# State space outputs by channels in a hybrid decoder layer: X as the left operand, z turned instead of y, and the norm's factor in the addition to h

## The chip, the cores and the metric

The kernel runs on one core of one Trainium2 chip. Times are microseconds of that core on the device, from the first to the last instruction of one execution with what the runtime counts around it; the figure that is compared is the median of several runs. TensorE is called PE, VectorE DVE, ScalarE ACT, GpSimd POOL and SyncE, which issues most transfers, SP.

## The reference

One layer of a decoder over T = 256 tokens of width 2048. All values are float32.

```
a    = RMSNorm(h)
[z | x,B,C | dt | q | k | v] = a @ W_in
x,B,C = SiLU(causal depthwise conv, 4 taps)
SSD  : per chunk of 128 tokens, group g (4), head (8 per group, 64 channels each):
         X      = x * dt
         a_cs   = cumsum(dt * A)                      along the chunk
         y_diag = (C B^T * exp(a_cs[l] - a_cs[s]) for s <= l) @ X
         state  = B^T @ (X * exp(a_cs[last] - a_cs))  of the chunk before
         y_off  = exp(a_cs) * (C @ state)             second chunk only
       y = y_diag + y_off + d_skip * x ;  y = y * SiLU(z)
       y = y * rsqrt(mean(y^2 over the group's 512 channels) + eps) * gain
Attn : per-head RMSNorm of q and k, rotary, window of 128, sinks
h    = h + concat(y, attention) @ W_out
h    = h + (SiLU(g) * u) @ W_down,  [g | u] = causal conv(RMSNorm(h) @ W_up)
h    = h + sigmoid(RMSNorm(h) @ W_pg) * RMSNorm(p @ W_pe)
```

## The kernel before

Every product with a weight matrix is made of three TensorE products of a number format that is faster than float32: each operand is split into a high and a low part, and hi*hi, hi*lo and lo*hi are added. So each weight tile of 128 x 1024 (`w`) is loaded, its high part `wh` is made on ACT and its low part `wl` on DVE, and PE takes 12 products of 512 columns from it. There are seven raw weight buffers and four split ones. The left operands (`ah`/`al` for the layer's normed input, `yh`/`yl` for the inputs to W_out) hold channels on partitions, tokens along the row; a product has 128 tokens on PSUM partitions and 512 columns.

The kernel has four stages: a load phase (some 55 us), in which the input and the first weights arrive and B and C are projected; the state space stage; attention with the rest of the output projection; and the two feed-forward parts. In the load phase the loop over `k` (16 steps, line 835) issues on SP, at step 8, four small loads after each other: `wd`, `scw`, `rows` and `posi` (lines 853 to 856); at steps 5 and 9 it loads the two halves of h, and ACT squares each as it lands (line 862).

The state space stage is not issued in the order in which it is written. `Recorder` notes every operation with its operands (all of these instructions carry line 341 in the profile), `cost` gives each an assumed duration, and `solve` lists them per engine by due times; then they are issued in that fixed order. `ORDER` names the steps in the order in which they are recorded: `x0` (chunk of x of group 0, its convolution, decays and outputs), `z0` (its gate), `e0` (gate, norm and split of the result), `o0` (its part of the output projection), `r0` (rotary tables), `k0` (projection of the keys). Groups 1 to 3 go to W_out during attention.

In `ssd_x` a chunk comes out of PE with tokens on partitions. The convolution wants channels on partitions, so `turned` splits the 32-bit words into 16-bit halves on ACT (`half`), turns them with a transposing transfer (`SY.dma_start_transpose`), and joins them on ACT. After convolution and SiLU, `xc` is turned back in the same way. From it come `yc` = x * d_skip and `Xd` = x * dt, tokens on partitions. The products of a chunk are:

```
PE.matmul(yp[:, hs], lhsT=segs[c][:, h, :], rhs=Xd[c][:, hs], start=True, stop=True)   # 8 heads
PE.matmul(off, lhsT=CT[:, g, c * P : (c + 1) * P], rhs=prev, start=True, stop=True)    # second chunk
```

`segs` are the decays times C B^T, 128 x 128 a head; `prev` is the state of the first chunk. These are float32 products, two TensorE instructions each. `y` thus has tokens on partitions. `ssd_end` multiplies it by the gate, squares it on ACT with a sum along the row, scales it by the factor, turns it with two transposing transfers, and splits it with the gain as a per-partition scale. `TURNED` says what of x (`x`), of `xc` on the way back (`b`) and of y (`y`) is turned by transfers; `KEYS_DMA` says the same of B and C. B is turned by eight PE transposes, C by transfers.

Of the kernel before, what the change touches and what calls it, by code (L numbers as in the profile page):

```python
# [12 lines left out]
F32 = mybir.dt.float32  # L13
# [41 lines left out]
ROUNDS = 6  # L55
GBUF = 3
TAPS = (0,)
TURNED = ("xby", "xby", "xby", "xby")
KEYS_DMA = (False, True)
ORDER = "x0 r0 x1 z0 e0 x2 z1 e1 x3 o0 z2 e2 z3 e3 k0".split()  # L60
GATE_SECOND = [0, 1, 2, 3, 4, 5, 6, 7]


# [432 lines left out]
def cost(engine, method, args, kw, outs, ins):  # L496
    n = size(outs[0])
    if engine == "PE":
        if method == "transpose":
            return 0.11, 0.0  # L500
        if kw["lhsT"].dtype == F32R:
            return 0.0128 + 0.00042 * n, 0.0
        return 2 * max(0.105, 0.013 + 0.00042 * n), 0.0
    if engine == "SP":
        if method == "dma_start_transpose":
            return 1.0, 6.5
        return max(0.5, 2.0 * n / 1024), 2.2
# [18 lines left out]
def hybrid_layer(  # L526
# [122 lines left out]

    scw = sb(mc, [P, 24 * 5], "scw")  # L650
    rw = sb(mc, [P, 256], "rows")
    dtb, alog, dsk, sink = (rw[:, i * 32 : (i + 1) * 32] for i in range(4))
    qg, kg_ = rw[:, 128:192], rw[:, 192:256]
    g_attn, g_ffn, g_ple, g_ssm = (gn[:, i * KT : (i + 1) * KT] for i in range(4))
# [1 line left out]
    fcw = sb(const, [P, 88 * 4], "fcw")  # L656
    fill(mc)

    def rstd(ss, n, cols, tag):
        t = sb(small, [P, cols], "rs_t")  # L660
        V.tensor_scalar(t, ss, 1.0 / n, EPS, op0=ALU.mult, op1=ALU.add)
        r = sb(small, [P, cols], tag)
        G.tensor_tensor(out=r, in0=t, in1=nhalf[:, :cols], op=ALU.pow)
        return r

# [138 lines left out]
    def v3(a, m):  # L804
        return a.rearrange("p (a b) -> p a b", a=m)
# [7 lines left out]
    with xin_:  # L813
# [21 lines left out]
        for k in range(KT):  # L835
# [16 lines left out]
            if k == 8:  # L852
                nc.sync.dma_start(wd, w_dt)
                nc.sync.dma_start(scw, ssm_cw)
                nc.sync.dma_start(rw, rows.partition_broadcast(P))
                nc.sync.dma_start(posi, pos)
                split(wd, dhl[:, :, :32], dhl[:, :, 32:])
            if k in (5, 9):
# [26 lines left out]
            res.append(t)  # L885
        return res

    def add_to_h(acc, n):
        for b in range(NB):
            hs = hres[b][:, n * NC : (n + 1) * NC]  # L890
            V.tensor_tensor(out=hs, in0=hs, in1=acc[b], op=ALU.add)

    def squares(ss, n):

# [10 lines left out]
        V.tensor_reduce(out=s1, in_=ss, axis=AX.X, op=ALU.add)  # L905
        return rstd(s1, D, NB, tag)

    def project(lhs, w, i0, ni, after=None):

        for n in range(4):  # L910
            acc = acc_pair()
            gemm(acc, lhs, [w[i, n] for i in range(i0 * KG // KW, (i0 + ni) * KG // KW)])
            add_to_h(acc, n)
            if after:
                after(n)


    held = {}
# [3 lines left out]
    with tc.tile_pool(name="ssd", bufs=1) as sp, tc.tile_pool(name="dram", bufs=1, space=bass.MemoryType.DRAM) as dp:  # L922
# [32 lines left out]
        def turned(ts, tags):  # L955
            u = sb(sp, [P, 4, T], "uc")
# [53 lines left out]
        scr = plan.tile(dp, [64, P], "scr", lambda: dp.tile([64, P], F32, tag="scr", name="scr"), 1)  # L1010
        SY.dma_start(scr, acsT)
        eacs = sb(sp, [P, 64], "eacs")
        S.activation(out=eacs, in_=acs, func=AF.Exp)

        def ssd_x(g):
            segs = []
# [37 lines left out]
            y, Xd = [], []  # L1054
            for b in range(NB):
                yc = sb(sp, [P, NC], f"yc{b}", bufs=2)
# [18 lines left out]
            S.copy(prev, st)  # L1075
            for c in range(NB):
                yc = y[c]
                yp = ms_tile()
                with pe_group():
                    for h in range(8):  # L1080
                        hs = slice(h * HD, (h + 1) * HD)
                        PE.matmul(yp[:, hs], lhsT=segs[c][:, h, :], rhs=Xd[c][:, hs], start=True, stop=True)
                V.tensor_tensor(out=yc, in0=yc, in1=yp, op=ALU.add)
                if c:
                    off = ms_tile()
                    PE.matmul(off, lhsT=CT[:, g, c * P : (c + 1) * P], rhs=prev, start=True, stop=True)
                    t = sb(sp, [P, NC], "xe")
                    o = g * 16 + 8
                    V.tensor_tensor(out=v3(t, 8), in0=v3(off, 8), in1=bc(eacs[:, o : o + 8], HD), op=ALU.mult)
                    V.tensor_tensor(out=yc, in0=yc, in1=t, op=ALU.add)  # L1090
            return y

        def ssd_gate(g):
            acc = in_chunk(3 + 2 * g)
            zs = []
            for b in range(NB):
                z = sb(sp, [P, NC], f"z{b}")
                S.activation(out=z, in_=acc[b], func=AF.Silu, scale=rx[:, b : b + 1])
                zs.append(z)
            return zs  # L1100

        def ssd_end(g, y, zs):
            ssy = sb(sp, [P, NB], "ssy", bufs=2)
            for b in range(NB):
                V.tensor_tensor(out=y[b], in0=y[b], in1=zs[b], op=ALU.mult)
                S.activation(out=zs[b], in_=y[b], func=AF.Square, accum_out=ssy[:, b : b + 1])
            ry = rstd(ssy, NC, NB, "ry")
            for b in range(NB):
                V.tensor_scalar_mul(y[b], y[b], ry[:, b : b + 1])
            yT = Lhs(yp_, KG, "y")  # L1110
            gain = g_ssm[:, 4 * g : 4 * g + 4]
            if "y" in TURNED[g]:
                u = turned(y, ("z", "Xd"))
                for f in range(4):
                    h, l = yT.part(f)
                    split(u[:, f, :], h, l, gain[:, f : f + 1])
            else:
                transpose_split(y, yT, 0, gain)
            return (yT, w_out, g, 1)

        def rotary():
            rp = sp
# [53 lines left out]
            S.activation(out=cos_t, in_=kk, func=AF.Sin)  # L1176
            return sin_t, cos_t

        ys, zs = {}, {}
        for step in ORDER:  # L1180
            what, g = step[0], int(step[1])
# [26 lines left out]
    with tc.tile_pool(name="att_s", bufs=2) as as_, tc.tile_pool(name="att", bufs=2, reuse_waits="tile") as ap_, tc.tile_pool(name="ps_sc", bufs=1, space=PSUM) as ps_sc:  # L1208
        plan = Recorder(zip(("DVE", "ACT", "POOL", "PE", "SP"), real_engines), {AF.Exp}, before.rest, before)
        V, S, G, PE, SY = plan.V, plan.S, plan.G, plan.PE, plan.SY  # L1210
        keys_acc = [plan.carry(t, (ps_acc, f"acc{b}")) for b, t in enumerate(keys_acc)]
        for lhs, *_ in held.values():
            lhs.t = [tuple(plan.carry(t, (yp_, f"y{e}0"), F32R) for e, t in zip("hl", ts)) for ts in lhs.t]
        aT.t = [tuple(plan.keep(t, [P, KG, T], act, f"a{e}{g}", 1, dtype=F32R) for e, t in zip("hl", ts)) for g, ts in enumerate(aT.t)]
        hres = [plan.keep(t, [P, D]) for t in real_h]
        early = [tuple(plan.carry(t, (wp, f"w{e}"), F32R) for e, t in zip("hl", ts)) for ts in early]
# [132 lines left out]
        def values(j):  # L1349

            yT = Lhs(yp_, KG, "y")
            for b in range(NB):
# [17 lines left out]
            held[4 + j] = (yT, w_out, 4 + j, 1)  # L1370

        def chunk(c, then):
            acc = acc_pair()
# [5 lines left out]
                yield  # L1379

        def output(i):
            lhs, w, i0, ni = held.pop(i)
            for n in range(4):
                acc = acc_pair()
                for s in range(2):
                    products(acc, lhs, load_w(w[i0 * 2 + s, n]), s * KW, KW, KG, s == 1)
                    if s == 1:
                        add_to_h(acc, n)
                    yield

        at = {}
# [820 lines left out]
```

## Time and profile before

| what | us |
|---|---|
| median of 3 runs | 1386.87 (1386.06 to 1386.89) |
| the profiled execution, its own time | 1387.34 |
| its span, first to last instruction | 1385.5 |
| PE busy | 1377.7 |
| DVE busy | 1212.3 |
| ACT busy | 1043.5 |
| POOL busy | 129.7 |

The span is divided among the engines as the table says; they work side by side, so the rows don't add up. Matmuls overlap in TensorE's pipeline: the mean duration of one is longer than the distance from one start to the next, and it is the distance that counts. "PE" rows are the products, "PEld" rows the loads of their left operand. A form such as `128*64 128x256` has 128 rows and 64 columns of left operand and 128 rows and 256 columns of moving operand. "SPq" is SP issuing a transfer; the time until it has landed is a "DMA" piece. In the chain of waits, each row is a start, a length and what it was.

### The profile page before, as it was taken

What the parts mean: (1) busy time and instruction counts of PE and PEld (TensorE: products, weight loads), DVE (VectorE), ACT (ScalarE), POOL (GpSimd) and SP (SyncE); (2) the same over time, 40 slices, a digit from 0 to 9 for tenths busy, and PEclk for the clock granted to TensorE, in tenths of its full rate; (3) what the DMA queues carried; (4) which work ended last, traced back from release to release, by engine and by line L of the source; (5) the groups of instructions that cost most, each with busy time, mean ns of one, the idle gap of its engine ahead of it and who ended that gap; (6) DMA issues with size and microseconds to landing.
All of it is one profiled execution on the core that took longest, in us unless ns stands there. A gap on an engine that the chain in (4) does not pass through costs nothing.

```text
span 1385.5 us, 18203 instructions
## 1 busy us (share of the span) xinstructions
PE 1377.7 (99%) x6270; PEld 1129.2 (82%) x6270; DVE 1212.3 (87%) x1591; ACT 1043.5 (75%) x1411; POOL 129.7 (9%) x113
## 2 busy tenths in 40 slices
PE   9999999999999999999999999999999999999998
PEld 7888888888787778888888888888888888888886
DVE  5779788676788897699999999999999999977999
ACT  6699897664677766587997886878688777868963
POOL 0002010027055332000000000000000000000000
PEclk9999999999999999999999999999999999999999
DMA  9778768668687778587868767676877678688762
GB/s 336 255 234 243 221 201 217 207 206 242 182 230 198 213 216 214 186 240 218 243 206 232 235 186 242 210 233 205 224 218 219 213 210 246 189 258 255 208 226 92
DMA packets 199852, 305.21 MB, mean 220 GB/s; under 512 B 127120, under 2 KB 129744, under 8 KB 199504
## 3 DMA queue, kind: packets, MB, share of 16 engines
q1 hardware_dynamic: 199328, 303.57, 73.5%
q8 instruction: 49, 0.80, 0.2%
q10 hardware_dynamic: 432, 0.48, 0.1%
q14 instruction: 43, 0.35, 0.1%
HBM read 270.41 MB, written 4.23 MB: 198 GB/s over the span
## 4 chain that ended last, share of the span: by engine, by line
PE 94%; DVE 3%; DMA 2%; issue 0%; ACT 0%; SPq 0%; DVEq 0%; ACTq 0%
PE acc L341 35%; PE b L1537 18%; PE b L1539 18%; PE b L1538 18%; PE ms L341 2%; PE acc L824 1%; PE tr L341 1%; PE sc L341 1%; DVE wl L1495 1%; DMA w<-in_w_in_dram 1%; DMA h<-in_x_dram 1%; DMA xt<-in_xT_dram 1%; DVE c L2095 0%; DVE c L2094 0%; PE b L1637 0%
## 5 line engine op out<-in xcount | busy, mean ns | idle before, releaser
L1491 ACT CAST wh<-w 128x1024 fp32r<-128x1024 f32 x296 | 308.4, 1051 | 129.6 <-PE b L1539 96.0
L1495 DVE TENSOR_TENSOR wl<-w,wh 128x1024 fp32r<-128x1024 f32 x296 | 355.7, 1219 | 38.6 <-ACT wh L1491 37.5
L341 DVE TENSOR_TENSOR wl<-w,wh 128x1024 fp32r<-128x1024 f32 x180 | 244.5, 1368 | 80.3 <-ACT wh L341 79.5
L341 ACT CAST wh<-w 128x1024 fp32r<-128x1024 f32 x180 | 188.0, 1049 | 124.8 <-PE acc L341 113.1
L341 PE MATMUL acc<-wh,ah 128*128 128x512 f32 x448 | 178.2, 398 | 0.0
L341 PE MATMUL acc<-wh,al 128*128 128x512 f32 x448 | 174.5, 390 | 0.0
L341 PE MATMUL acc<-wl,ah 128*128 128x512 f32 x448 | 174.4, 389 | 0.0
L1537 PE MATMUL b<-wh,gh 128*128 128x512 f32 x398 | 154.9, 389 | 0.0
L1539 PE MATMUL b<-wh,gl 128*128 128x512 f32 x398 | 154.8, 389 | 0.0
L1538 PE MATMUL b<-wl,gh 128*128 128x512 f32 x398 | 154.8, 389 | 0.0
L1539 PE MATMUL b<-wh,al 128*128 128x512 f32 x362 | 140.9, 389 | 0.0
L1537 PE MATMUL b<-wh,ph 128*128 128x512 f32 x352 | 137.1, 390 | 0.0
L1539 PE MATMUL b<-wh,pl 128*128 128x512 f32 x352 | 137.0, 389 | 0.0
L1538 PE MATMUL b<-wl,ph 128*128 128x512 f32 x352 | 136.9, 389 | 0.0
L1537 PE MATMUL b<-wh,ah 128*128 128x512 f32 x346 | 134.7, 389 | 0.0
L1538 PE MATMUL b<-wl,ah 128*128 128x512 f32 x346 | 134.7, 389 | 0.0
L341 PE MATMUL acc<-wh,yh 128*128 128x512 f32 x256 | 101.4, 396 | 0.0
L341 PEld LDWEIGHTS acc<-wh,ah 128*128 128x128 f32 x448 | 84.1, 188 | 19.5 <-issue 2.1
L341 PE MATMUL acc<-wl,yh 128*128 128x512 f32 x256 | 99.8, 390 | 0.0
L341 PE MATMUL acc<-wh,yl 128*128 128x512 f32 x256 | 99.6, 389 | 0.0
L341 PEld LDWEIGHTS acc<-wl,ah 128*128 128x128 f32 x448 | 84.2, 188 | 18.4 <-issue 1.4
L341 PEld LDWEIGHTS acc<-wh,al 128*128 128x128 f32 x448 | 84.1, 188 | 17.8
(290 smaller groups left out, 2514.9 us busy)
## 6 DMA issues: line engine op xcount, KB each, us to landing
w<-in_w_up_dram SPq DMA_DIRECT2D x176, 512.0 KB, 4.2
w<-in_w_in_dram SPq DMA_DIRECT2D x126, 512.0 KB, 4.5
w<-in_w_down_dram SPq DMA_DIRECT2D x88, 512.0 KB, 4.5
w<-in_w_out_dram SPq DMA_DIRECT2D x64, 512.0 KB, 4.2
w<-in_w_pg_dram SPq DMA_DIRECT2D x32, 512.0 KB, 4.1
seg<-scr SPq DMA_DIRECT2D x8, 512.0 KB, 4.9
xt<-in_xT_dram SPq DMA_DIRECT2D x16, 128.0 KB, 7.1
h<-in_x_dram SPq DMA_DIRECT2D x2, 1024.0 KB, 8.9
```

What stands on the lines that cost most here:

```text
L341: getattr(real, method)(*(concrete(a) for a in args), **{k: concrete(a) for k, a in kw.items()})
L824: PE.matmul(acc[b], lhsT=aT(k, b)[part % 2], rhs=wt[:, c, :], start=(k == 0 and not part), stop=(k == KT - 1 and part == 2))
L1491: S.copy(o.h, src.t)
L1495: V.tensor_tensor(out=o.l, in0=src.t, in1=o.h.bitcast(F32), op=ALU.subtract)
L1537: PE.matmul(t, lhsT=hi, rhs=wh, start=first, stop=False)
L1538: PE.matmul(t, lhsT=hi, rhs=wl, start=False, stop=False)
L1539: PE.matmul(t, lhsT=lo, rhs=wh, start=False, stop=last)
```

## The change

The outputs of the state space part are made with channels on partitions from the start.

- The diagonal products take `Xd` of a head (128 x 64) as the left operand and its decays (128 x 128) as the moving one. Even heads write PSUM partitions 0 to 63, odd heads 64 to 127.
- The inter-chunk product takes `prev` as the left operand, in four pieces of 128 channels, and C as the moving one. Its factor exp(a_cs) now runs along the row: it is written to DRAM once (`escr`) and loaded broadcast over 64 partitions, twice a group (`grown`).
- The skip term is `xc` itself, scaled on ACT by a per-partition column. The columns `dskT` are loaded in the load phase, after `rows`, by two loads with a stride of two elements.
- `z` is turned instead of `y`: SiLU on the way out of PSUM, then `turned`.
- The sum of squares runs over partitions: one squaring on ACT, two additions on DVE, and two matmuls with a column of -0.5 (the mean's scale takes the sign back).
- The factor of the norm is no longer applied to y, but in the addition to h after the projection, which becomes a `scalar_tensor_tensor`. Attention's parts have no factor.
- B is turned by transfers, as C was. The order of recording moves x1, x2 and x3 one step later each. The planner's assumed durations of float32 products change.

```diff
-TURNED = ("xby", "xby", "xby", "xby")
-KEYS_DMA = (False, True)
-ORDER = "x0 r0 x1 z0 e0 x2 z1 e1 x3 o0 z2 e2 z3 e3 k0".split()
+TURNED = ("xb", "xb", "xb", "xb")
+KEYS_DMA = (True, True)
+ORDER = "x0 r0 z0 e0 x1 z1 e1 x2 z2 e2 x3 o0 z3 e3 k0".split()
...
-        return 2 * max(0.105, 0.013 + 0.00042 * n), 0.0
+        narrow = min(kw["lhsT"].shape[0], outs[0].shape[0]) <= HD
+        return (max(0.107, 0.00084 * n) if narrow else max(0.21, 0.00168 * n)), 0.0
...
                 nc.sync.dma_start(rw, rows.partition_broadcast(P))
+                for e in range(2):
+                    nc.sync.dma_start(dskT[e * HD : (e + 1) * HD, :], rows[64 + e : 96 : 2].partition_broadcast(HD))
                 nc.sync.dma_start(posi, pos)
...
-    def add_to_h(acc, n):
+    def add_to_h(acc, n, factor=None):
         for b in range(NB):
             hs = hres[b][:, n * NC : (n + 1) * NC]
-            V.tensor_tensor(out=hs, in0=hs, in1=acc[b], op=ALU.add)
+            if factor is None:
+                V.tensor_tensor(out=hs, in0=hs, in1=acc[b], op=ALU.add)
+            else:
+                V.scalar_tensor_tensor(out=hs, in0=acc[b], scalar=factor[:, b : b + 1], in1=hs, op0=ALU.mult, op1=ALU.add)
...
         SY.dma_start(scr, acsT)
-        eacs = sb(sp, [P, 64], "eacs")
-        S.activation(out=eacs, in_=acs, func=AF.Exp)
+        eacsT = sb(sp, [64, P], "eacsT")
+        S.activation(out=eacsT, in_=acsT, func=AF.Exp)
+        SY.dma_start(escr, eacsT)
...
-                V.tensor_tensor(out=v3(yc, 8), in0=v3(src, 8), in1=bc(dsk[:, g * 8 : (g + 1) * 8], HD), op=ALU.mult)
-                y.append(yc)
                 V.tensor_tensor(out=v3(t, 8), in0=v3(src, 8), in1=bc(dt4[:, g, b, :], HD), op=ALU.mult)
                 Xd.append(t)
+            for f in range(4):
+                S.activation(out=xc[:, f, :], in_=xc[:, f, :], func=AF.Copy, scale=dskT[:, 4 * g + f : 4 * g + f + 1])
+            grown = sb(sp, [P, 4, P], "grown", bufs=1)
+            for e in range(2):
+                o = g * 16 + 8
+                SY.dma_start(grown[e * HD : (e + 1) * HD], escr[o + e : o + 8 : 2, :].partition_broadcast(HD))
...
                     for h in range(8):
-                        hs = slice(h * HD, (h + 1) * HD)
-                        PE.matmul(yp[:, hs], lhsT=segs[c][:, h, :], rhs=Xd[c][:, hs], start=True, stop=True)
-                V.tensor_tensor(out=yc, in0=yc, in1=yp, op=ALU.add)
+                        e = h % 2
+                        PE.matmul(
+                            yp[e * HD : (e + 1) * HD, h // 2 * P : (h // 2 + 1) * P],
+                            lhsT=Xd[c][:, h * HD : (h + 1) * HD],
+                            rhs=segs[c][:, h, :],
+                            start=True,
+                            stop=True,
+                        )
+                V.tensor_tensor(out=yc, in0=xc[:, :, c * P : (c + 1) * P], in1=v3(yp, 4), op=ALU.add)
                 if c:
                     off = ms_tile()
-                    PE.matmul(off, lhsT=CT[:, g, c * P : (c + 1) * P], rhs=prev, start=True, stop=True)
+                    with pe_group():
+                        for f in range(4):
+                            fs = slice(f * P, (f + 1) * P)
+                            PE.matmul(off[:, fs], lhsT=prev[:, fs], rhs=CT[:, g, c * P : (c + 1) * P], start=True, stop=True)
...
-            return zs
+            return turned(zs, ("half", "z"))
-        def ssd_end(g, y, zs):
...
+        def ssd_end(g, y, z):
+            V.tensor_tensor(out=y, in0=y, in1=z, op=ALU.mult)
+            S.activation(out=z, in_=y, func=AF.Square)
+            V.tensor_tensor(out=z[:, :2, :], in0=z[:, :2, :], in1=z[:, 2:, :], op=ALU.add)
+            V.tensor_tensor(out=z[:, 0, :], in0=z[:, 0, :], in1=z[:, 1, :], op=ALU.add)
+            ss = ms_tile()
+            with pe_group():
+                for b in range(NB):
+                    PE.matmul(ss[:, b * 8 : (b + 1) * 8], lhsT=z[:, 0, b * P : (b + 1) * P], rhs=nhalf[:, :8], start=True, stop=True)
+            ry = factors[:, g * NB : (g + 1) * NB]
+            rstd(ss[:, : NB * 8].rearrange("p (b n) -> p b n", b=NB)[:, :, 0], -0.5 * NC, NB, "", ry)
             yT = Lhs(yp_, KG, "y")
-            gain = g_ssm[:, 4 * g : 4 * g + 4]
...
+            for f in range(4):
+                h, l = yT.part(f)
+                split(y[:, f, :], h, l, g_ssm[:, 4 * g + f : 4 * g + f + 1])
+            return (yT, w_out, g, 1, ry)
```

More of the change, by code (lines that the diff above doesn't have):

```diff
@@ L651, in hybrid_layer @@
     rw = sb(mc, [P, 256], "rows")
+    dskT = sb(mc, [P, KT], "dskT")
     dtb, alog, dsk, sink = (rw[:, i * 32 : (i + 1) * 32] for i in range(4))
@@ L657, in hybrid_layer, with rstd @@
     fill(mc)
-    def rstd(ss, n, cols, tag):
+    def rstd(ss, n, cols, tag, r=None):
         t = sb(small, [P, cols], "rs_t")
         V.tensor_scalar(t, ss, 1.0 / n, EPS, op0=ALU.mult, op1=ALU.add)
-        r = sb(small, [P, cols], tag)
+        r = sb(small, [P, cols], tag) if r is None else r
         G.tensor_tensor(out=r, in0=t, in1=nhalf[:, :cols], op=ALU.pow)
@@ L906, in finish_rstd, with project @@
         return rstd(s1, D, NB, tag)
-    def project(lhs, w, i0, ni, after=None):
+    def project(lhs, w, i0, ni, factor=None):
         for n in range(4):
@@ L912, in project @@
             gemm(acc, lhs, [w[i, n] for i in range(i0 * KG // KW, (i0 + ni) * KG // KW)])
-            add_to_h(acc, n)
-            if after:
-                after(n)
+            add_to_h(acc, n, factor)
     held = {}
@@ L953, in turn, with turned @@
             S.copy(dst.bitcast(U16).rearrange("p c (t a) -> p c t a", a=2), flip.rearrange("p (a c) t -> p c t a", a=2))
-        def turned(ts, tags):
-            u = sb(sp, [P, 4, T], "uc")
+        def turned(ts, tags, tag="uc"):
+            u = sb(sp, [P, 4, T], tag)
             for b in range(NB):
@@ L1009, in hybrid_layer @@
         V.tensor_copy(acsT, ps[:64, :P])
-        scr = plan.tile(dp, [64, P], "scr", lambda: dp.tile([64, P], F32, tag="scr", name="scr"), 1)
+        scr, escr = (plan.tile(dp, [64, P], t, lambda t=t: dp.tile([64, P], F32, tag=t, name=t), 1) for t in ("scr", "escr"))
         SY.dma_start(scr, acsT)
-        eacs = sb(sp, [P, 64], "eacs")
-        S.activation(out=eacs, in_=acs, func=AF.Exp)
+        eacsT = sb(sp, [64, P], "eacsT")
+        S.activation(out=eacsT, in_=acsT, func=AF.Exp)
+        SY.dma_start(escr, eacsT)
         def ssd_x(g):
@@ L1053, in ssd_x @@
             S.activation(out=xc, in_=xc, func=AF.Silu)
[L1054 removed]
+            Xd = []
             for b in range(NB):
[L1056 removed]
                 t = sb(sp, [P, NC], f"Xd{b}")
@@ L1075, in ssd_x @@
             S.copy(prev, st)
+            y = sb(sp, [P, 4, T], "y", bufs=2)
             for c in range(NB):
-                yc = y[c]
+                yc = y[:, :, c * P : (c + 1) * P]
                 yp = ms_tile()
@@ L1080, in ssd_x @@
                     for h in range(8):
-                        hs = slice(h * HD, (h + 1) * HD)
-                        PE.matmul(yp[:, hs], lhsT=segs[c][:, h, :], rhs=Xd[c][:, hs], start=True, stop=True)
-                V.tensor_tensor(out=yc, in0=yc, in1=yp, op=ALU.add)
+                        e = h % 2
[7 more added lines that the diff above has]
+                V.tensor_tensor(out=yc, in0=xc[:, :, c * P : (c + 1) * P], in1=v3(yp, 4), op=ALU.add)
                 if c:
                     off = ms_tile()
-                    PE.matmul(off, lhsT=CT[:, g, c * P : (c + 1) * P], rhs=prev, start=True, stop=True)
+                    with pe_group():
+                        for f in range(4):
+                            fs = slice(f * P, (f + 1) * P)
+                            PE.matmul(off[:, fs], lhsT=prev[:, fs], rhs=CT[:, g, c * P : (c + 1) * P], start=True, stop=True)
                     t = sb(sp, [P, NC], "xe")
-                    o = g * 16 + 8
-                    V.tensor_tensor(out=v3(t, 8), in0=v3(off, 8), in1=bc(eacs[:, o : o + 8], HD), op=ALU.mult)
-                    V.tensor_tensor(out=yc, in0=yc, in1=t, op=ALU.add)
+                    V.tensor_tensor(out=v3(t, 4), in0=v3(off, 4), in1=grown, op=ALU.mult)
+                    V.tensor_tensor(out=yc, in0=yc, in1=v3(t, 4), op=ALU.add)
             return y
@@ L1099, in ssd_gate @@
                 zs.append(z)
-            return zs
-        def ssd_end(g, y, zs):
[L1103 to L1109, printed above, removed]
-            yT = Lhs(yp_, KG, "y")
-            gain = g_ssm[:, 4 * g : 4 * g + 4]
[L1112 to L1119, printed above, removed]
+            return turned(zs, ("half", "z"))
[10 more added lines that the diff above has]
+            rstd(ss[:, : NB * 8].rearrange("p (b n) -> p b n", b=NB)[:, :, 0], -0.5 * NC, NB, "", ry)
+            yT = Lhs(yp_, KG, "y")
+            for f in range(4):
+                h, l = yT.part(f)
+                split(y[:, f, :], h, l, g_ssm[:, 4 * g + f : 4 * g + f + 1])
+            return (yT, w_out, g, 1, ry)
         def rotary():
@@ L1177, in rotary @@
             return sin_t, cos_t
+        factors = sb(const, [P, 4 * NB], "factors")
         ys, zs = {}, {}
@@ L1211, in hybrid_layer @@
         keys_acc = [plan.carry(t, (ps_acc, f"acc{b}")) for b, t in enumerate(keys_acc)]
-        for lhs, *_ in held.values():
+        for i, (lhs, w, i0, ni, ry) in held.items():
             lhs.t = [tuple(plan.carry(t, (yp_, f"y{e}0"), F32R) for e, t in zip("hl", ts)) for ts in lhs.t]
+            held[i] = lhs, w, i0, ni, plan.keep(ry.real(), [P, NB], at=before.left([u[0] for u in ry.tile.uses if u[3]]))
         aT.t = [tuple(plan.keep(t, [P, KG, T], act, f"a{e}{g}", 1, dtype=F32R) for e, t in zip("hl", ts)) for g, ts in enumerate(aT.t)]
@@ L1369, in values @@
                 split(v3(o, 4), hi, lo)
-            held[4 + j] = (yT, w_out, 4 + j, 1)
+            held[4 + j] = (yT, w_out, 4 + j, 1, None)
         def chunk(c, then):
@@ L1381, in output @@
         def output(i):
-            lhs, w, i0, ni = held.pop(i)
+            lhs, w, i0, ni, factor = held.pop(i)
             for n in range(4):
@@ L1387, in output @@
                     if s == 1:
-                        add_to_h(acc, n)
+                        add_to_h(acc, n, factor)
                     yield
```

## The prediction

> **What bounds the kernel now.** First the page: busy shares and the chain.
>
> ```profile
> PE 1377.7 (99%) x6270; PEld 1129.2 (82%) x6270; DVE 1212.3 (87%) x1591; ACT 1043.5 (75%) x1411; POOL 129.7 (9%) x113
> PE 94%; DVE 3%; DMA 2%; issue 0%; ACT 0%; SPq 0%; DVEq 0%; ACTq 0%
> ```
>
> TensorE is busy 99% of the span and is 94% of the chain that ends last. So a microsecond of TensorE work taken out is worth a microsecond, and another engine counts only where it makes TensorE wait. Next, the stage that is changed, in the table by stretches.
>
> ```profile
> 55.00:250.00 195.00, 195.00 (x917) 160.86 (x916) 167.41 (x267) 173.67 (x210) 15.50 (x10) 1.00 0.76 222
> 110.00:120.00 10.00, 10.00 (x46) 8.29 (x45) 9.97 (x9) 9.97 (x11) 4.49 (x3) 1.00 0.81 217
> ```
>
> The columns are length, then PE, PEld, DVE, ACT and POOL. PE is never idle at a clock of 1.00; ACT has 195.0 - 173.7 = 21.3 us free over the stage and nothing in the stretch from 110 to 120, where DVE is full too. That PE does not stop there shows that the four split buffers ahead of it carry it over such a burst. Last, the chain of waits through the load phase, with SP's own timeline and waits.
>
> ```profile
> 13.14 8.75 DMA w<-in_w_in_dram
> 21.90 0.38 SPq L622
> 22.32 7.97 DMA h<-in_x_dram
> 30.37 1.87 ACT xs L862
> ...
> 35.03 4.83 PE acc L824 x20
> 54.56 0.87 PE tr L341 x8
> 16.13 0.33 SPq L853 DMA_DIRECT2D wd<-in_w_dt_dram  x1
> 19.01 0.43 SPq L855 DMA_DIRECT2D rows<-in_rows_dram  x1
> 20.23 0.33 SPq L856 DMA_DIRECT2D posi<-in_pos_dram  x1
> 60.98 1.35 SPq L341 DMA_TRANSPOSE Xd<-half  x1
> SPq L854 <- DMA h<-in_x_dram: 2.2, 1, 2.2
> SPq L856 <- DMA w<-in_w_in_dram: 0.8, 1, 0.8
> wd<-in_w_dt_dram SPq DMA_DIRECT2D x1, 256.0 KB, 8.0
> ```
>
> Here the chain is not PE's: the second half of h, issued at 22.32, lands at 30.29, ACT squares it, and only behind that stand the splits that PE waits for at 35.03. That transfer has no slack.
>
> **The change, part by part.**
>
> *Diagonal products (64 of them, 8 to a chunk of 128 rows).* Each matmul is two instructions. How long a group holds PE I read as the distance between the weight products on its two sides, less the products' own time (0.227 us each: 456 of them take 103.41).
>
> ```profile
> 255.01 103.41 PE acc L341 x456
> 122.87 0.39 PE L341 MATMUL acc<-wh,al 128*128 128x512 f32 x1
> 123.10 1.89 PE L341 MATMUL ms<-Xd,seg 128*128 128x64 f32 x16
> 124.83 1.08 PE L341 MATMUL ms<-xe,Bt 128*128 128x512 f32 x2
> ...
> 125.97 0.39 PE L341 MATMUL acc<-wl,ah 128*128 128x512 f32 x1
> 358.03 0.39 PE L341 MATMUL acc<-wh,al 128*128 128x512 f32 x1
> 358.35 1.16 PE L341 MATMUL sc<-kT,qT 64*128 64x128 f32 x16
> 359.44 0.50 PE L341 MATMUL acc<-wh,ah 128*128 128x512 f32 x1
> 359.77 0.39 PE L341 MATMUL acc<-wl,ah 128*128 128x512 f32 x1
> 416.21 0.39 PE L341 MATMUL acc<-wh,yl 128*128 128x512 f32 x1
> 416.52 2.81 PE L341 MATMUL tr<-s,v 128*64 128x256 f32 x24
> 419.27 0.50 PE L341 MATMUL acc<-wh,yh 128*128 128x512 f32 x1
> 419.61 0.40 PE L341 MATMUL acc<-wl,yh 128*128 128x512 f32 x1
> ```
>
> Before: 16 instructions in 124.83 - 123.10 = 1.73 us, 0.108 each, and about 0.03 of edge. The new form, 64 columns of left operand and 128 moving, does not occur. Its nearest rows are attention's. The values (128*64, alternating column halves as the change does) run 24 instructions over 256 columns; 419.61 - 416.21 - 0.45 = 2.95 us in all. At 0.107 each 2.57 of that is streaming and 0.38 is edge: going into and out of the half-array form costs TensorE something that the full form does not pay. Half the columns gives 16 x 0.054 + 0.38 = 1.24. The scores (16 instructions over 128 columns, row halves) hold PE 359.77 - 358.03 - 0.45 = 1.29. I take 1.26: a gain of 0.50 a chunk, 4.0 us for eight. Ends: 1.09 (from 358.35 to 359.44, were the way into and out of the form hidden), 0.67 x 8 = 5.4 us gained; and 1.48 (the values' 2.95 halved, edges and all), 2.3.
>
> The row says that column halves run beside each other. The Trainium skill, page "TensorE: Matmul & The Clock Gate", part 3, "The mechanism", holds that a weight load overlaps running matmuls only where the row group differs, and column halves share theirs. By that each instruction would pay its load (about 53 ns for 64 columns, an estimate from that page's P/1.2) on top of its stream of 0.108, the diagonal would lose 6.5 us where the rows gain 4.0, and the sum would end near 1396. The trace does not bear it out: the values' 24 loads lie inside their 2.75 us.
>
> *The inter-chunk product* becomes four matmuls of 128 columns in place of one of 512. The latter is two instructions as st is; from 124.83, two of those and a weight product end at 125.97, 1.14 - 0.23 = 0.91. Four small ones are eight instructions.
>
> ```profile
> 133.69 0.39 PE L341 MATMUL acc<-wh,al 128*128 128x512 f32 x1
> 133.92 0.60 PE L341 MATMUL ms<-CT,BT 128*128 128x128 f32 x4
> ...
> 134.60 0.40 PE L341 MATMUL acc<-wl,ah 128*128 128x512 f32 x1
> ```
>
> These four hold PE 134.60 - 133.69 - 0.45 = 0.46, so eight 0.9: no change.
>
> *Sum of squares over channels* is new on PE: two matmuls a group, four instructions whose left operand is as large as in the row above: 0.46 x 4 groups = +1.8 us. Ends: 0.9, half of it, if a stream of 8 columns is cheaper than one of 128, and 3.3, if each paid the half-array form's 0.38 besides. I take the row, since its loads are the same. They are placed by a plan that lets products go ahead of them; what stands behind them on PE, should they be late, is the stream of weight products itself. The factor that they give, before a scaling of y ahead of its split (0.48 a half on DVE), now waits for no one but the addition to h, a whole projection later.
>
> *B turned by DMA:* its eight PE transposes go, 0.87 us (54.56). PE has weight products to put there.
>
> *ACT.* Rows of the stage:
>
> ```profile
> L341 ACT COPY uc<-ct 128x1024 uint16<-128x1024 uint16 x8 | 9.2, 1170 | 0.2 <-DVE yl L341 0.2
> L341 ACT COPY half<-xc 128x1024 uint16<-128x1024 uint16 x8 | 8.3, 1043 | 0.1
> L341 ACT ACTIVATE z<-yc 128x512 f32<-128x512 f32 x6 | 3.8, 627 | 0.0
> L341 ACT ACTIVATION_READ_ACCUMULATOR z<-yc 128x1 f32 x6 | 1.1, 187 | 0.0
> L341 ACT ACTIVATE yh<-uc,gains 128x256 fp32r<-128x256 f32 x8 | 3.4, 498 | 0.1
> L341 DVE TENSOR_TENSOR yc<-Xd,rows 128x512 f32<-128x512 f32 x8 | 5.5, 686 | 0.6 <-ACT Xd L341 0.6
> L341 DVE TENSOR_SCALAR yc<-yc,ry 128x512 f32<-128x512 f32 x5 | 2.3, 484 | 3.1 <-POOL ry L341 3.1
> ```
>
> Turning B adds 2 x (1.04 + 1.17) = 4.4; the skip term, 16 scalings of 256 at 0.50, 8.0; the squares lose 8 x (0.63 + 0.19) = 6.5 and come back as four of 1024, about 1.05 each as a copy of that size, 4.2. Turning z for y is even. Net +10.1 us, hidden by the 21.3 free; without that cover it would be PE's loss. DVE loses 8 x 0.69 and 8 x 0.48 and gains two additions a group (0.69 + 0.4): -5.0. The 32 additions to h become three-operand ones; between nothing and 0.2 dearer each (the gap of the two DVE rows), 6.4 us in all at the most, of which the eight of this stage stand against 195.0 - 167.4 = 27.6 us that DVE has free. POOL keeps its four powers.
>
> *Order:* x1, x2 and x3 move one chunk later, past z0, z1 and z2; ACT's heavy bursts spread, and the PE sum is unchanged. What is new is that z3's squares must reach PE before attention starts: four copies 4.4 us, two activations, a product, a square and two sums at about 1 each, a transfer of at most 8 (the longest landing above), some 18 us, behind k0's 96 products x 0.227 = 21.8. I cost it at nothing; with ACT full it would be late by what ACT is late, which is the second rival's price. SP issues 11 more transfers in the stage (2 transposes at 1.35, one write of exponentials, 8 loads of them). The raw weights have seven buffers, 19 us of products, between them and PE, so I cost these at nothing; uncovered, they would be 2.7 us for the transposes and 9 x 0.43 = 3.9 for the rest.
>
> *Skip columns:* two strided loads join SP's queue between rows (19.01) and posi (20.23), ahead of the load of h at 22.32 that has no slack. SP's waits look like eight transfers in flight: L854 waits for the h load eight issues ahead, L856 for the w eight ahead, the w at 21.90 for that of 13.14. Two more push each later issue's wait two places on: h then waits for wd, 16.13 + 8.0 = 24.1 in place of 22.32, +1.8 us straight onto PE. Ends: 0 if bandwidth makes up for it (less than nothing is excluded, they only add), 2.7 if each also holds SP as a transpose does (1.35). I take 1.8, from the row of the very transfer waited for. By the Trainium skill, "DMA: Bandwidth & Descriptors", "Rules for kernel authors", a strided last dimension lowers to one descriptor an element; 2048 of them at that page's 10.5 ns over 16 engines would be an estimated 1.3 us more, ending at 1386.9; no run shows it.
>
> **Sum:** -4.0 + 0 + 1.8 - 0.9 + 1.8 = -1.3 us. Against the profiled execution (span 1385.5, 1387.34 in all, 0.47 over the median of 1386.87) that is 1386.0; on the median, 1385.6. About 0.2% (2.8 us) is what a measurement can tell from no change.
>
> **The rivals.**
> *Loads hidden.* If h lands at 30.3 as now, only PE's -3.1 stays: 1383.8, down to 1382.4 with the cheaper edges. For it: landing takes 8 us, with room to make up; against: the two waits on SP.
> *ACT becomes the bound (slower).* ACT's 21.3 free become 21.3 - 10.1 - 3.1 = 8.1, 4% of the stage. It decides once a split of weights comes later than the buffers ahead of PE last. If half the added 10.1 falls in full stretches like 110 to 120, PE loses 5.0 on top of the sum: 1390.6. Against: the new order thins these stretches.
> *The halves run one after the other.* Then a group costs 1.73 + 0.38 = 2.11, 8 x 0.35 = 2.8 lost in place of 4.0 gained: 1392.4. The values' row speaks against it: one after the other, 24 passes over 256 columns would take 24 x 0.22 = 5.3 us (twice the 0.11 of the row of CT), not 2.75. The page's rule on weight loads belongs here as well, and the same row speaks against it.
>
> **How the numbers follow.** Forecast 0.53 (own range 1384.2 to 1387.3, the ends of the diagonal), loads hidden 0.25, ACT 0.19, halves in turn 0.03. Of the hidden loads 0.20 lies beyond 0.2%, of the forecast 0.06: faster 0.26. Slower takes ACT's 0.17 and the halves' 0.03: 0.20. Same 0.54. The range from 1382.6 to 1389.6 leaves out the halves, ACT's upper half and the cheapest edges.
>
> **What would show it.** A diagonal group of 16 instructions of form 128*64 within 1.3 us; four small groups of squares at 0.46; no transposes near 54; h issued after 24 and PE's wait at 35 longer by 1.8; ACT above 90% between 55 and 250 with PE still full. Wrong if PE shows idle time between 60 and 290, or if h lands as early as now.

## The result: 18 us slower, all of it lost before the state space stage begins

| | before | after |
|---|---|---|
| median, us | 1386.88 (1386.06 to 1387.69) | 1404.41 (1403.97 to 1405.05) |
| ratio | 1 | 1.0127 (95% interval 1.0109 to 1.0144) |
| span of the profiled execution | 1385.5 | 1402.1 |

The forecast was 1385.6 with a range up to 1389.6: the time lies 14.8 us above the range. The page of the changed kernel, busy shares and chain:

```profile
PE 1376.8 (98%) x6302; PEld 1125.5 (80%) x6302; DVE 1208.9 (86%) x1579; ACT 1045.8 (75%) x1414; POOL 133.0 (9%) x113
PE 89%; DVE 5%; DMA 2%; ACT 1%; issue 1%; SPq 1%; ACTq 0%; DVEq 0%
```

PE is busy 0.9 us less than before in a span that is 16.6 us longer, so PE has gained idle time. Where it lies is told by the waits of PE up to 330 us:

```profile
PE acc L826 <- ACT wh L670: 17.0, 2, 15.7
```

The same wait in the kernel before, where the loop is line 824:

```profile
PE acc L824 <- ACT wh L668: 0.2, 1, 0.2
```

The columns are the total, the number of waits and the longest. One wait of 15.7 us is nearly the whole loss, and it is in the load phase (line 826 is the projection loop there). The chain in that stretch says what ACT itself waited for:

```profile
13.54 8.58 DMA w<-in_w_in_dram
22.14 8.24 SPq L860
30.48 3.68 SPq L618
34.21 11.80 DMA w<-in_w_in_dram
46.11 1.05 ACT wh L670
47.21 10.82 PE acc L826 x36
```

Of the 34 us from 13.54 to 47.21, 12 are SP issuing two transfers and 11.8 the landing of a weight tile. SP's own timeline shows what stands just ahead of the long issues:

```profile
20.47 1.46 SPq L859 DMA_DIRECT2D dskT<-in_rows_dram  x2
22.14 8.24 SPq L860 DMA_DIRECT2D posi<-in_pos_dram  x1
30.48 3.68 SPq L618 DMA_DIRECT2D xt<-in_xT_dram  x1
...
34.69 0.90 SPq L864 DMA_DIRECT2D h<-in_x_dram  x1
```

Line 859 is the two strided loads of the skip columns. SP issues them in 0.7 us each; it is the issue behind them, 1 KB of positions, that takes 8.24 us where it took 0.33. The load of h goes out at 34.69 in place of 22.32. Their landing, with the times of the two issues (20.5 and 21.2), and that of the positions behind them:

```profile
L859 SPq DMA_DIRECT2D dskT<-in_rows_dram x2: 686/705/724, 20.5 to 21.2; - x2
DMA to landing us min/median/max: 12.8/17.9/22.9
```

```profile
posi<-in_pos_dram SPq DMA_DIRECT2D x1, 1.0 KB, 22.2
```

Each load brings 64 partitions 16 numbers of 4 bytes, 1024 pieces and 4 KB. The first lands at 20.5 + 12.8 = 33.3 and the second at 21.2 + 22.9 = 44.1: 10.8 us for 1024 pieces, 10.5 ns apiece. The table by stretches (length, PE, PEld, DVE, ACT, POOL, granted clock, DMA share, GB/s) shows that hardly anything else moved meanwhile:

```profile
20.00:22.00 2.00, 2.00 (x10) 1.65 (x10) 0.48 (x1) 2.00 (x4) 0.00 (x0) 1.00 1.06 402
36.00:38.00 2.00, 0.00 (x0) 0.00 (x0) 0.00 (x0) 0.00 (x0) 0.00 (x0) 0.50 0.05 0
44.00:46.00 2.00, 0.00 (x0) 0.00 (x0) 0.48 (x1) 0.51 (x1) 0.00 (x0) 0.50 1.07 419
```

From 402 GB/s to nothing, with the DMA engines busy 5% of the time: they are neither full nor free. At 44 to 46, when the second load has landed, the bytes flow at 419 GB/s again. From 26 to 36 us the packets are these small pieces and nothing else (the kernel before moved 366 GB/s in the same 10 us):

```profile
DMA packets 1078, 0.00 MB, mean 0 GB/s; under 512 B 1078, under 2 KB 1078, under 8 KB 1078
```

That is 9.3 ns a piece, somewhat less than between the landings. A share of 5% is also what one DMA engine of 16, nearly full, would show while 15 stand free. The trace speaks against that: it has 16 landing signals for each of these transfers, and of the 1 KB of positions, whose issue is over at 30.37, the first comes at 40.01. Every part of that transfer stood behind the pieces.

The clock column of the table shows a second price: after some microseconds without products TensorE is granted 0.50 (it is 1.00 up to 34 us and 0.50 from 36 on), and the first products after the wait run at that clock.

```profile
47.21 1.22 PE L826 MATMUL acc<-wh,ah 128*128 128x512 f32 x2 [15.66 <-ACT wh L670]
48.23 1.05 PE L826 MATMUL acc<-wh,al 128*128 128x512 f32 x2
49.08 1.05 PE L826 MATMUL acc<-wl,ah 128*128 128x512 f32 x2
...
52.20 0.63 PE L826 MATMUL acc<-wh,ah 128*128 128x512 f32 x2
...
72.56 0.39 PE L341 MATMUL acc<-wh,ah 128*128 128x512 f32 x1
```

Two products take 0.85 us from start to start (48.23 to 49.08), where two take 0.46 at full clock. From 52.20 the pace is normal again, so the 12 products before that took 5.0 us in place of 12 x 0.227 = 2.7: some 2.3 us more. The state space stage starts at 72.56 (its first product) instead of 55.19: 17.4 us later. The span is 16.6 us longer. All behind that point is thus 0.8 us shorter than before.

### The profile page after: what moved, and what is told of

Read it like the earlier page. It is cut to its first block, busy times and chain, and to the rows that moved or that the text cites. A ratio compares the mean times of both kernels' runs of the same rounds, so it can differ in the third digit from the quotient of the medians.

```text
span 1402.1 us, 18292 instructions
## 1 busy us (share of the span) xinstructions
PE 1376.8 (98%) x6302; PEld 1125.5 (80%) x6302; DVE 1208.9 (86%) x1579; ACT 1045.8 (75%) x1414; POOL 133.0 (9%) x113
## 4 chain that ended last, share of the span: by engine, by line
PE 89%; DVE 5%; DMA 2%; ACT 1%; issue 1%; SPq 1%; ACTq 0%; DVEq 0%
PE acc L341 31%; PE b L1556 18%; PE b L1555 18%; PE b L1557 18%; DMA w<-in_w_in_dram 2%; PE acc L826 2%; PE ms L341 1%; PE sc L341 1%; DVE wl L1513 1%; PE tr L341 1%; DVE wl L341 1%; SPq L860 1%; DVE xc L341 0%; SPq L618 0%; DVE c L2113 0%
## 5 line engine op out<-in xcount | busy, mean ns | idle before, releaser
L1513 DVE TENSOR_TENSOR wl<-w,wh 128x1024 fp32r<-128x1024 f32 x296 | 355.5, 1218 | 38.4 <-ACT wh L1509 37.5
L341 DVE TENSOR_TENSOR wl<-w,wh 128x1024 fp32r<-128x1024 f32 x180 | 238.1, 1328 | 72.4 <-ACT wh L341 70.8
L341 ACT CAST wh<-w 128x1024 fp32r<-128x1024 f32 x180 | 188.2, 1049 | 125.6 <-PE acc L341 109.8
L341 PE MATMUL acc<-wh,ah 128*128 128x512 f32 x448 | 176.4, 394 | 0.0
L341 PE MATMUL acc<-wh,al 128*128 128x512 f32 x448 | 174.5, 390 | 0.0
L341 PE MATMUL acc<-wl,ah 128*128 128x512 f32 x448 | 174.4, 389 | 0.0
L341 PE MATMUL acc<-wh,yh 128*128 128x512 f32 x256 | 101.5, 396 | 0.0
L341 PE MATMUL acc<-wl,yh 128*128 128x512 f32 x256 | 99.8, 390 | 0.0
L341 PE MATMUL acc<-wh,yl 128*128 128x512 f32 x256 | 99.7, 389 | 0.0
L341 PEld LDWEIGHTS acc<-wh,ah 128*128 128x128 f32 x448 | 84.1, 188 | 18.7 <-issue 1.3
L341 PEld LDWEIGHTS acc<-wh,al 128*128 128x128 f32 x448 | 84.1, 188 | 17.7
L341 PEld LDWEIGHTS acc<-wl,ah 128*128 128x128 f32 x448 | 84.2, 188 | 16.9
```

The costliest lines, as they stand in the source:

```text
L341: getattr(real, method)(*(concrete(a) for a in args), **{k: concrete(a) for k, a in kw.items()})
L1513: V.tensor_tensor(out=o.l, in0=src.t, in1=o.h.bitcast(F32), op=ALU.subtract)
```

## The experiments

Theories at the outset: the two loads cost what the forecast's queue arithmetic says (1.8 us) and the loss is elsewhere in the change; or the loads make the whole loss, by their number of small pieces, by the way they read, by where they write, or by their place in SP's queue. Each run is a median, with its ratio to the kernel before on the same chip; the before's median was 1386.97, 1387.08 and 1387.04 on the three chips.

**1 (e1_copies). The change without the two loads.** The columns are made by DVE from the row that is already on chip.

```diff
-                for e in range(2):
-                    nc.sync.dma_start(dskT[e * HD : (e + 1) * HD, :], rows[64 + e : 96 : 2].partition_broadcast(HD))
...
+        for e in range(2):
+            V.tensor_copy(dskT[e * HD : (e + 1) * HD, :], dsk[e * HD : (e + 1) * HD, e::2])
```

> The changed kernel without the two strided loads; the skip columns are copied by two DVE instructions from the rows that are in SBUF already. Theory A (the 4-byte pieces of the strided loads cost the 18 us, the rest of the change is worth what PE's sum says): h lands near 30 again, PE's wait in the load phase falls from about 18 to about 2 us, and the time is 1404.4 - 18 - (1 to 2 for the slow clock after the stall) = 1383.5 to 1386. Theory B (something else in the change holds the load phase, say the new schedule): still above 1395.

Measured: 1385.81, ratio 0.999 (0.9981 to 0.9999), span 1383.5. The loads cost 1404.4 - 1385.8 = 18.6 us. The load of h goes out at 21.63 and the chain through the load phase is that of before:

```profile
21.63 8.30 DMA h<-in_x_dram
...
34.67 4.84 PE acc L826 x20
```

**2 (e3_before_strided). The kernel before, with the two loads alone** (their result is used by nothing).

```diff
+    dskT = sb(mc, [P, KT], "dskT")
...
+                for e in range(2):
+                    nc.sync.dma_start(dskT[e * HD : (e + 1) * HD, :], rows[64 + e : 96 : 2].partition_broadcast(HD))
```

> The kernel before with nothing but the two strided loads added, their result unused. Theory A: the whole loss is there without the rest of the change: 1386.9 + 16 to 20 = 1403 to 1407. Theory B (the rest of the change makes the load phase slow): under 1390.

Measured: 1406.6, 1.0141 (1.0128 to 1.0155): +19.6 us. The same wait is there (here ACT's line is 669):

```profile
PE acc L825 <- ACT wh L669: 16.7, 2, 16.3
```

So the loss needs nothing else of the change: the two loads are enough, and without them there is none.

**3 (e2_plain). Two plain loads in the same place:** each partition reads 16 numbers that lie side by side, 128 pieces of 64 bytes in all.

```diff
-                    nc.sync.dma_start(dskT[e * HD : (e + 1) * HD, :], rows[64 + e : 96 : 2].partition_broadcast(HD))
+                    nc.sync.dma_start(dskT[e * HD : (e + 1) * HD, :], rows[64 + e * 16 : 80 + e * 16].partition_broadcast(HD))
```

> The two loads stay where they are, but each takes 16 neighbouring elements (64 bytes in one piece) in place of 16 elements at a stride of two, so the skip term takes other heads' factors. Theory A (pieces): 128 pieces in place of 2048, so nearly all of the loss goes: within 2.5 us of e1. My prediction's reading (two more issues in a ring of eight transfers): e1 + 1.8 us. A theory that the loads cost by being broadcasts over 64 partitions: still above 1395.

The skip term takes other heads' factors here, so the result is not the layer's. Measured: 1387.42, 1.0006 (0.9997 to 1.0015): 1.6 us over the first experiment. SP's timeline:

```profile
21.48 0.33 SPq L860 DMA_DIRECT2D posi<-in_pos_dram  x1
...
23.78 0.93 SPq L864 DMA_DIRECT2D h<-in_x_dram  x1
```

The load of h goes out 2.15 us later than in the first experiment, much as the forecast's reading of eight transfers in flight has it (1.8). That step was right for two ordinary issues; the other 17 us come from what is inside these two.

**4 (e4_one_strided). One strided load in place of two,** the other half by a copy.

```diff
+                nc.sync.dma_start(dskT[:HD, :], rows[64:96:2].partition_broadcast(HD))
...
+        V.tensor_copy(dskT[HD:, :], dsk[HD:, 1::2])
```

> The changed kernel with one of the two strided loads; the other half of the columns is copied on DVE. Theory A with a cost per piece: half the pieces, and the part of it that the loads in flight can hide comes off first: 6 to 9 us over e1. A theory of a threshold (a queue that overflows only with the second load): within 2 us of e1.

Measured: 1394.72, 1.0057 (1.0041 to 1.0072): 8.9 us over the first experiment, about half of 18.6. It landed after 14.7 us, and now it is h's own issue that is held:

```profile
22.74 4.09 SPq L863 DMA_DIRECT2D h<-in_x_dram  x1
```

**5 (e5_act_queue). The loads from ACT's queue,** so that SP has nothing of them to issue.

```diff
-                    nc.sync.dma_start(dskT[e * HD : (e + 1) * HD, :], rows[64 + e : 96 : 2].partition_broadcast(HD))
+                    nc.scalar.dma_start(dskT[e * HD : (e + 1) * HD, :], rows[64 + e : 96 : 2].partition_broadcast(HD))
```

> The two strided loads are issued on ACT's queue in place of SP's, at the same step. Theory A1 (each piece is slow on the transfer engines, and only the queue that it stands in waits for it): SP's loads pass beside it, h lands within 2 us of its time in e1, and the whole is within 3 us of e1. Theory A2 (a transfer engine is held by each piece, whatever queue it is from): SP's loads are held as before, 1398 or more. Theory C (SP's issuing is what is slow): SP is free, near e1.

Measured: 1404.77, 1.0127 (1.0113 to 1.0141), no better. ACT's queue lets them go in the first microseconds (at 1.55 and 2.27), and SP's issues stall there instead; the table by stretches shows the same dead time from 10 us on (43 GB/s or less from 8 to 22 us):

```profile
3.82 5.59 SPq L618 DMA_DIRECT2D xt<-in_xT_dram  x1
9.46 6.24 SPq L623 DMA_DIRECT2D w<-in_w_in_dram  x1
16.36 4.95 SPq L618 DMA_DIRECT2D xt<-in_xT_dram  x1
```

```profile
2.00:4.00 2.00, 2.00 (x6) 0.73 (x5) 0.51 (x2) 0.73 (x2) 0.64 (x3) 1.00 0.97 274
10.00:12.00 2.00, 0.00 (x0) 0.00 (x0) 0.00 (x0) 0.00 (x0) 0.00 (x0) 0.86 0.17 43
```

SP's queue holds none of the pieces here and is held all the same. What they occupy is shared by the queues. The Trainium skill, page "DMA: Bandwidth & Descriptors", section "Rules for kernel authors", says that spreading transfers over issuing engines doesn't help, as all run on the same 16 DMA engines; this run agrees (1404.77 against 1404.41).

**6 (e8_spread). Written 64 bytes apart** (into a wider tile, from which DVE copies the column), to see whether 16 pieces for one stretch of on-chip memory are what collides.

```diff
+                dw = sb(xin, [P, KT, 16], "dw")
...
-                    nc.sync.dma_start(dskT[e * HD : (e + 1) * HD, :], rows[64 + e : 96 : 2].partition_broadcast(HD))
+                    nc.sync.dma_start(dw[e * HD : (e + 1) * HD, :, 0], rows[64 + e : 96 : 2].partition_broadcast(HD))
...
+        V.tensor_copy(dskT, dw[:, :, 0])
```

> The same 2048 pieces of 4 bytes from the same addresses, but written 64 bytes apart in SBUF, into a wider tile from which DVE copies the columns at the end of the load phase. If the slowness comes from neighbouring writes of 4 bytes into the same line of SBUF, they now go as fast as posi's pieces, and the time is within 3 us of e1. If each 4-byte piece is slow wherever it is written, 1402 to 1406 as in the changed kernel.

Measured: 1404.71, 1.0127 (1.0113 to 1.0141). No change, so it is not where they write.

**7 (e9_spread_only). Read side by side, written 64 bytes apart:** as 6, from the contiguous source of 3. The pieces are again 4 bytes, without a stride in the source.

```diff
-                    nc.sync.dma_start(dskT[e * HD : (e + 1) * HD, :], rows[64 + e : 96 : 2].partition_broadcast(HD))
+                    nc.sync.dma_start(dw[e * HD : (e + 1) * HD, :, 0], rows[64 + e * 16 : 80 + e * 16].partition_broadcast(HD))
```

> The source is 16 neighbouring elements, as in e2, but they are written 64 bytes apart, so the pieces are 2048 of 4 bytes again (the skip term takes other heads' factors). If it is the cutting into pieces that costs, whichever side asks for it: 1402 to 1406. If it is reading at a stride: within 3 us of e2's 1387.4.

The skip term again takes other heads' factors. Measured: 1403.52, 1.0118 (1.0105 to 1.0132). The stride of the source is not needed: it is enough that the broadcast falls into 2048 pieces of 4 bytes.

**8 (e11_other_source). As many pieces, from rows of their own.** The first experiment with two more loads of 1024 pieces of 4 bytes with the same stride, in which each partition reads its own row of x instead of 64 partitions the same 128 bytes.

```diff
+                dw = sb(xin, [P, KT], "dw")
...
+                    nc.sync.dma_start(dw[e * HD : (e + 1) * HD, :], x[0][e * HD : (e + 1) * HD, : 2 * KT : 2])
```

> e1 with two strided loads of 1024 pieces of 4 bytes into an unused tile, not broadcast: each partition reads its own row of x. If each piece holds a transfer engine for about 0.15 us, 1403 to 1407. If it is that 64 partitions read the same 128 bytes of memory over and over: within 3 us of e1 (1385.8 + 1.6).

Measured: 1388.48, 1.001 (1.0001 to 1.0019), 2.7 us over the first experiment and some 1 over the plain loads, with an interval about as wide. The landing of the two loads, and the issue behind them on SP:

```profile
DMA to landing us min/median/max: 4.7/4.8/5.0
```

```profile
21.21 2.66 SPq L861 DMA_DIRECT2D posi<-in_pos_dram  x1
```

The same number of pieces of the same size lands within 5.0 us of its issue instead of 22.9, and the issue behind them takes 2.66 in place of 8.24. Being cut up costs little; being cut up and read by 64 partitions from the same 128 bytes costs much. One more thing differs between the two: the broadcast steps through its source by zero from partition to partition, and rows of their own don't. The two were not parted.

**9 (e13_pairs). The same broadcast in pieces of 8 bytes,** 1024 in all, beside the first experiment.

```diff
+                dw = sb(xin, [P, 8, 2], "dw")
...
+                    nc.sync.dma_start(dw[e * HD : (e + 1) * HD], rows[64:96].rearrange("(n a) -> n a", a=4)[:, :2].partition_broadcast(HD))
```

> e1 with two strided loads, broadcast as in the change, in pieces of 8 bytes: 512 pieces each, 1024 in all, into an unused tile. The bytes are those of the change, the pieces half. Cost per piece: about +9 to +11 over e1, as e4 (1394 to 1397). Cost per byte or per load: as the changed kernel, 1402 or more.

Measured: 1394.25, 1.0053 (1.0038 to 1.0069): 8.4 us over the first experiment, as much as 1024 pieces of 4 bytes (8.9). The second landing is 12.7 - 7.6 + 0.7 (between the issues) = 5.8 us behind the first, 11.3 ns for each of its 512 pieces:

```profile
DMA to landing us min/median/max: 7.6/10.1/12.7
```

Between 4 and 8 bytes the price is by piece, not by byte.

**10 (e6_old_order). The old order of steps,** on the first experiment.

```diff
-ORDER = "x0 r0 z0 e0 x1 z1 e1 x2 z2 e2 x3 o0 z3 e3 k0".split()
+ORDER = "x0 r0 x1 z0 e0 x2 z1 e1 x3 o0 z2 e2 z3 e3 k0".split()
```

> e1 with the order of recording of the kernel before (x1 ahead of z0, and so on). PE's sum is the same; my prediction costs the order at nothing: within 1.5 us of e1. If the new order is what keeps ACT from stopping PE, PE waits appear between 60 and 200 and it is 2 to 6 us slower than e1. If the new order causes the two short waits of e1 (0.5 us of the sum of squares of group 0 on DVE, 0.3 us of xe), it is up to 1 us faster.

Measured: 1386.21, 0.9994 (0.9985 to 1.0003), span 1384.1. The intervals overlap. The waits of PE have moved, not grown by much:

```profile
PE tr L341 <- ACT Bt L341: 0.7, 1, 0.7
PE acc L341 <- DVE wl L341: 0.5, 1, 0.5
```

**11 (e7_b_by_pe). B by PE transposes as before,** on the first experiment.

```diff
-KEYS_DMA = (True, True)
+KEYS_DMA = (False, True)
```

> e1 with B turned by PE transposes again. By the sum, 0.87 us more on PE and 4.4 us less on ACT: e1 + 0.9. If ACT's load is what makes the waits of group 0 (0.8 us), they go and it is even.

Measured: 1385.08, 0.9986 (0.9977 to 0.9995), span 1383.9. It is the lowest median of all, though not told apart from the first experiment. In the stage, waits are gone: PE is busy 195.0 of the 195 us from 55 to 250, where the first experiment has 194.34. In the load phase it waits 0.8 us for `wh`, where the first experiment has 0.3, so what makes up for B's transposes on PE is not shown.

**12 (e12_order_and_b). Both of the last two.**

```diff
-KEYS_DMA = (True, True)
-ORDER = "x0 r0 z0 e0 x1 z1 e1 x2 z2 e2 x3 o0 z3 e3 k0".split()
+KEYS_DMA = (False, True)
+ORDER = "x0 r0 x1 z0 e0 x2 z1 e1 x3 o0 z2 e2 z3 e3 k0".split()
```

> e1 with both the old order and B by PE transposes. e6 waited on ACT for B's left operand near 86 (0.7 us) and on a weight split (0.5); with B by PE both should go: as e7 (1385.1) within 1 us. If the old order costs by itself, 1 us or more over e7.

Measured: 1385.95, 0.999 (0.9982 to 0.9999). No better than either; among these four versions (1385.1 to 1386.2) the differences are about what a measurement can tell.

## Why the prediction was wrong, step by step

*What failed: the skip columns.* The forecast put +1.8 us on the two loads, between 0 and 2.7, and they cost 18.6. The step that failed is the cost of the loads themselves, which it took as nothing: it counted them as two issues in a queue of eight, and for two issues the count was good (1.6 in experiment 3). It took a load of 4 KB to be as quick as the loads beside it, and bounded the price by rows of whole-row loads and transposes, none of which has a piece of 4 bytes read many times over. The upper end was therefore no bound. The price of the missing kind of transfer was unknown, and no row of before reached it. What the runs show in its place is a price by the piece for such a broadcast: 8.9 us for 1024 pieces (experiment 4), 18.6 for 2048.

The path was off as well. The forecast had the load of h hold up PE; h landed at 34.69 + 13.8 = 48.5, after PE had gone on at 47.21. What PE waited for was the weight tile that was issued at 34.21, behind the two long issues.

The forecast did have a sentence on the pieces: from a figure of the Trainium skill's page "DMA: Bandwidth & Descriptors" (section "Measured (HBM→SBUF, 128 partitions, SWDGE, issued from GpSimd)") it estimated 1.3 us for 2048 descriptors over 16 engines. That page of the Trainium skill gives its 10.5 ns a packet for a transfer of 64 packets as a whole. The division by 16 was the forecast's own step; without it the estimate from that page of the Trainium skill would have been 21.5 us. That this is close to what happened does not make the figure a price for any small piece: in experiment 8, 2048 of them had landed some 5.5 us after the first issue, at most 2.7 ns each. Here the measurement decides.

Two follow-on costs were not foreseen either: other transfers wait with the pieces (0 GB/s from 36 to 38), and TensorE comes back at a clock of 0.50.

*The rivals.* None of the three occurred. The slower case was put down to ACT becoming the bound. ACT had room: in the first experiment, 55 to 250 us,

```profile
55.00:250.00 195.00, 194.34 (x942) 158.16 (x941) 161.49 (x250) 176.15 (x220) 18.50 (x11) 1.00 0.86 233
```

ACT is at 176.15 of 195 us, 90.3%, as "above 90%" had it, with PE 99.7% busy. It has 2.5 us more to do than before, not 10.1, and part of the reason was not in the sum: loads of activation tables, from 49 to 258 us, in the kernel before and then in the first experiment:

```profile
L341 ACT ACT_TABLE_LOAD x16 | 20.5, 1283 | 1.6 <-DVE xc L341 1.3
```

```profile
L341 ACT ACT_TABLE_LOAD x11 | 14.1, 1283 | 0.8 <-DVE xc L341 0.6
```

Five fewer, 6.4 us. With the old order there are 14 (experiment 10) and with B on PE 13 (experiment 11), so the order and the way of turning B have a part in it; which activations spare a load was not traced. DVE came out as said: 161.49 against 167.41, -5.9 where -5.0 was forecast. The addition to h with the factor takes 0.744 us, inside the 0.2 that was allowed over the plain one:

```profile
L341 DVE SCALAR_TENSOR_TENSOR h<-acc,factors,h 128x512 f32<-128x512 f32 x8 | 5.6, 744 | 0.0
```

*What held: PE's terms.* Timeline of PE in the first experiment, one group's four products:

```profile
174.25 0.39 PE L341 MATMUL acc<-wh,al 128*128 128x512 f32 x1
174.47 1.02 PE L341 MATMUL ms<-xe,Bt 128*128 128x512 f32 x2
175.42 1.09 PE L341 MATMUL ms<-seg,Xd 128*64 128x128 f32 x16
176.45 0.50 PE L341 MATMUL acc<-wh,ah 128*128 128x512 f32 x1
176.79 0.39 PE L341 MATMUL acc<-wl,ah 128*128 128x512 f32 x1
...
179.08 0.39 PE L341 MATMUL acc<-wh,al 128*128 128x512 f32 x1
179.40 1.09 PE L341 MATMUL ms<-seg,Xd 128*64 128x128 f32 x16
180.42 1.16 PE L341 MATMUL ms<-CT,prev 128*128 128x128 f32 x8
181.34 0.48 PE L341 MATMUL acc<-wh,ah 128*128 128x512 f32 x1
181.65 0.39 PE L341 MATMUL acc<-wl,ah 128*128 128x512 f32 x1
```

By the forecast's own reading the first stretch holds PE 176.79 - 174.25 - 0.45 = 2.09 us and the second 181.65 - 179.08 - 0.45 = 2.12. With 0.91 for the state and 0.9 for the inter-chunk product, both as forecast, a diagonal is 1.20 (said: 1.26; before: 1.73). Eight of them gain 4.2 us where 4.0 was said. The column halves do run beside each other: 16 instructions of 128 columns in 1.03 us, 0.064 each, which leaves no place for the rival of halves in turn. The squares:

```profile
192.60 0.39 PE L341 MATMUL acc<-wh,al 128*128 128x512 f32 x1
192.84 0.51 PE L341 MATMUL ms<-nhalf,uc 128*128 128x8 f32 x4
...
193.51 0.39 PE L341 MATMUL acc<-wl,ah 128*128 128x512 f32 x1
```

193.51 - 192.60 - 0.45 = 0.46 a group, to the hundredth; a stream of 8 columns was no cheaper than the forecast's row of 128, with a left operand of the same size. What was missed is a wait: group 0's squares come 0.5 us late from DVE (`PE ms L341 <- DVE uc L341`, one wait), and that group's edges are wider too, 1.23 us in all. B's transposes bring the first product of the stage from 55.19 to 54.05, 1.1 us (said: 0.9).

*The sum without the loads:* -4.2 + 1.8 + 0.8 (group 0) - 1.1 = -2.7 of PE's time; the span of the first experiment is 2.0 us shorter and its median 1.2. The 0.7 between sum and span was not traced; the runs of that kernel lie between 1384.24 and 1386.69. That its median of 1385.81 falls beside the forecast's 1385.6 is chance: without the 1.8 for the loads the forecast's terms give 1383.8. Without its loads the change is thus just about what can be told from no change; with them, 18.6 us of loss cover it.

*What stays open.* Shown is that the cost needs many small pieces (3 against 7), goes by their number (4, 9), goes with 64 partitions reading the same 128 bytes rather than rows of their own (8), and does not depend on the queue (5), the place written (6) or the source's stride (7). Whether the step of zero or the shared bytes does it was not parted, and whether the line of memory, its channel, or the DMA engines' way of fetching it serves one read at a time can't be told from these traces.

The best version is the change with the skip columns copied on chip and B transposed on PE: 1385.08, 0.14% under before (0.05% to 0.23%).

## What to carry to other kernels

Count a small load by its pieces and by how many of them read the same bytes, not by its size: of 8 KB in 2048 pieces the second half took 22.9 us to land here, a weight tile of 512 KB 8.6 us, and the pieces stopped those as well. Where a small value is wanted in another arrangement on many partitions, load it once in long runs and rearrange it on chip; the DVE copies that did it left the load phase as it was. When a change adds a kind of transfer that no row of the profile shows, the nearest rows are not its bounds: leave the upper end open as far as the stage has no slack.

## What the hardware showed that was not expected

- 1024 pieces of 4 bytes read by 64 partitions from the same 128 bytes took 10.8 us from one landing to the next (10.5 ns each; 9.3 in the steady stretch from 26 to 36 us); 1024 of 8 bytes cost as much as 1024 of 4 (8.4 and 8.9 us). From rows of their own, 1024 pieces had landed within 5.0 us of their issue, and 2048 within some 5.5 us of the first.
- While they last, other transfers nearly stand still: 0 GB/s from 26 to 36 us on the same queue, with the DMA engines busy 5% of the time, and 43 GB/s or less from 8 to 22 us with the pieces on ACT's queue (SP's issues then took 5.59, 6.24 and 4.95 us).
- The stall halved the TensorE clock (0.50 from 36 to 50 us), and the first 12 products behind it took 0.42 us each instead of 0.23.
- Column halves with 64 columns of left operand run at 0.064 us an instruction, with some 0.2 us of edges around a group of 16.
